# Two token-mixing blocks on one core: which lower parts stand ahead of a handover, and who writes the upper part of a turned input

## The chip, the cores and the metric

The kernel runs on one core of a Trainium2 chip. The metric is the device time of one execution in microseconds (us). The engines are TensorE (PE; PEld is its weight load), VectorE (DVE), ScalarE (ACT), GpSimd (POOL) and SyncE (SP), which issues nearly all loads.

## The reference, cut to what matters

A sequence of 256 tokens of width 1024 goes through two blocks. The first: a gated feed-forward, a token mixing (retention and a neighbourhood attention) and a second gated feed-forward, each with an RMS norm ahead and behind. The second: two layers, each an attention and a feed-forward with a layer norm behind.

```
x = x + 0.5 * rms_norm(swiglu(rms_norm(x)))          # first block: ffn1, mixing, ffn2
...
for i in range(2):                                    # second block
    h = x * (1.0 + scale1) + shift1
    y = moba_attention(h) if i == 0 else diff_attention(h)
    x = layer_norm(ALPHA * x + (1.0 + gate1) * y)
    h = x * (1.0 + scale2) + shift2
    x = layer_norm(ALPHA * x + (1.0 + gate2) * sq_relu_mlp(h))
```

`scale`, `shift` and `gate` are six rows per layer, a product of `silu(c)` with the matrix `ada_w`, which is read along the way. All weights are read once, in float32.

## The kernel before, in words

**Upper and lower parts.** Every float32 operand of a matrix product is split in two: an upper part (a copy rounded to the matmul's format) and a lower part (the operand less the upper part). A product takes three matmuls: upper with upper, the weight's lower with the input's upper, and the weight's upper with the input's lower. For weights these are `wh` and `wl`, for the turned (transposed) input of a stage the two halves of `XX`.

**The weight stream** (class `Stream`). Weights come in slots of two halves of 128 x 1024. A half is loaded into one of 6 `raw` buffers; ScalarE writes `wh` (L115), VectorE `wl` (L93), each into a ring of 8 buffers. `piece` issues one `wh` and appends the half to the list `late`; `flush(n)` issues the open lower parts until `n` are left. A `raw` buffer is free for its next load once its lower part is done; loads are issued by SP in the order of the slots. `use(n)` is called by a stage ahead of its matmuls on slot `n`: it makes the pieces that are missing and then flushes the whole of `late`. `tick`, called after each half that TensorE has used up, makes up to two pieces and flushes.

**Handovers.** Each stage ends in `down_tail`: the last products are done bank by bank (two token halves t, two column halves f; a bank is 128 x 512), so that the norm of token half 0 can run while TensorE does half 1. After each bank, `post.bank` evacuates it. After the last one, `ahead(3)` makes three pieces without any lower part, and `flush(post.low)` issues lower parts until `low` are left: 2 behind an RMS norm (`PostRms`), 1 behind a layer norm (`PostLn`). The next stage begins with `projT`: `use` of its two slots, then for each token half `turn(t)`, which transposes the normed input on TensorE and writes both parts of `XX`, and 24 matmuls of 512 columns. `turn(0)` is already done in the tail (`mid`); `turn(1)` stands right behind it.

`turn_of` has two forms. Without a shift (`c is None`) ScalarE writes the upper part and VectorE the lower one, 128 columns at a time (L597, L598). With a shift ScalarE writes `hf` (L606, eight times); then, for groups of 2, 2 and 4 blocks of 128 columns, the upper part follows, by ScalarE for token half 0 (L612) and by VectorE for half 1 (L610), and the lower part by VectorE (L613).

There are six handovers with a `projT` behind them, numbered here as in the rest of the text: place 1, ffn1 to mixing; place 2, mixing to ffn2; place 3, ffn2 to the first attention; place 4, that attention to its feed-forward; place 5, feed-forward to the second attention; place 6, that attention to its feed-forward. Places 1 to 3 have an RMS norm ahead, 4 to 6 a layer norm; the turns of places 3 to 6 have a shift. Behind `projT`, an attention evacuates `q` by VectorE (L1230 and the lines behind it), a feed-forward of the second block evacuates `u` as `q` by ScalarE and VectorE (L765, L766) and transposes that on TensorE (L771).

Each engine runs its instructions in the order in which the program issues them (manual schedule), so a lower part that is issued early stands ahead of all later work of VectorE.

Of the kernel before, what the change touches and what calls it, by code (L numbers as in the profile page):

```python
# [12 lines left out]
AF = mybir.ActivationFunctionType  # L13
# [35 lines left out]
class Stream:  # L49
# [39 lines left out]

    def flush(self, n=0):  # L90
        while len(self.late) > n:
            wl, raw, wh = self.late.popleft()
            self.nc.vector.tensor_tensor(wl, raw, wh.bitcast(F32), OP.subtract)  # L93

    def next_pos(self):
# [7 lines left out]
    def piece(self, lag=1):  # L103
        nc, i, h = self.nc, self.si, self.half
        raw = self.raw.pop((i, h))
        self.half += 1
        if self.half == 2:
            self.half, self.si = 0, i + 1
        if self.seq[i][0] == "w":
            n = self.wpos[i]  # L110
            assert 2 * n + h < self.done + RING, (n, h, self.done)
            wh = self.pool.tile([128, 1024], F32R, name="wh", bufs=RING)
            wl = self.pool.tile([128, 1024], F32R, name="wl", bufs=RING)
            self.parts[n, h] = (wh, wl)
            nc.scalar.activation(wh, raw, AF.Copy)  # L115
            self.late.append((wl, raw, wh))
            if lag is not None:
                self.flush(lag)
            self.load_to()
        else:  # L120
            self.flush()
            self.ada(self.seq[i][3], h, raw)
            self.load_to()
# [32 lines left out]
    def use(self, n, b):  # L156

        while self.next_pos() <= n + 0.5:
            self.piece()
        self.flush()  # L160
        return [[t.rearrange("p (k f) -> p k f", f=b) for t in self.parts[n, h]] for h in range(2)]

    def release(self, n, h):
# [8 lines left out]
def block_kernel(ctx, tc, A, out):  # L172
    nc = tc.nc
    V, SC, PE, GP = nc.vector, nc.scalar, nc.tensor, nc.gpsimd
# [14 lines left out]
    def w2(name, bufs=None):  # L189
        return work.tile([128, 512], F32, name=name, tag="w2", bufs=4)  # L190
# [395 lines left out]
    def turn_of(src, a, c, alloc=gu):  # L586

        def turn(t):
            ps = [alloc("xt"), alloc("xt")]
            for k in range(8):  # L590
                PE.transpose(ps[k // 4][:, k % 4 * 128:k % 4 * 128 + 128], src[:, t, k * 128:(k + 1) * 128], ident)
            if c is None:
                for i in range(4):
                    for b in range(2):
                        k = 4 * b + i
                        x, h, l = ps[b][:, i * 128:(i + 1) * 128], XX[:, k, 0, TS[t]], XX[:, k, 1, TS[t]]
                        SC.activation(h, x, AF.Copy, scale=a[:, k:k + 1])  # L597
                        V.scalar_tensor_tensor(l, x, a[:, k:k + 1], h.bitcast(F32), op0=OP.mult, op1=OP.subtract)  # L598
                return
            for k0, n in ((0, 2), (2, 2), (4, 4)):  # L600
                if k0 != 2:
                    w = w2("hf").rearrange("p (k s) -> p k s", k=4)
                f = w[:, k0 % 4:k0 % 4 + n]
                for i in range(n):
                    k = k0 + i
                    SC.activation(f[:, i], ps[k // 4][:, k % 4 * 128:k % 4 * 128 + 128], AF.Identity,  # L606
                                  scale=a[:, k:k + 1], bias=c[:, k:k + 1])
                h, l = (XX[:, k0:k0 + n, i, TS[t]] for i in range(2))
                if t:
                    V.tensor_copy(h, f)  # L610
                else:
                    SC.activation(h, f, AF.Copy)  # L612
                V.tensor_tensor(l, f, h.bitcast(F32), OP.subtract)  # L613
        return turn

    class PostRms:

        low = 2
# [19 lines left out]

    class PostLn:

        low = 1

        def __init__(self, accs, gate):
            self.accs, self.gate = accs, gate
# [846 lines left out]
```

## Time and profile before

| | us |
|---|---|
| median of 3 runs | 1288.45 (1286.58 to 1289.17) |
| profiled execution, own time | 1282.29 |
| its span | 1280.3 |
| TensorE busy | 1234.5 (96%) |
| VectorE busy | 932.7 (73%) |
| ScalarE busy | 642.5 (50%) |
| of these, lower parts L93 on VectorE, 392 of them | 467.0 |
| of these, upper parts L115 on ScalarE, 392 of them | 400.2 |

The median is of whole executions, the rows are of one profiled execution. In the chain of work that ended last TensorE has 83%, VectorE 8% (half of it the lower parts, 4%) and ScalarE 3%. A row of a timeline gives the start, the time from the first start to the last end of the merged instructions, engine, line and operation, output and inputs, the count, and in brackets the idle time ahead of it with what ended it.

### The profile page before, as it was taken

Reading aid. Unit: us, or ns where it says so; the run is one execution under the profiler, and the core shown is the slowest. Engines: PE = TensorE matmul, PEld = TensorE weight load, DVE = VectorE, ACT = ScalarE, POOL = GpSimd, SP = SyncE. Lnnn points to the kernel's source line nnn. Section 1 sums busy time; section 2 is a strip of 40 time slices with the busy share of each in tenths; the row PEclk is TensorE's granted clock in tenths of the full one; section 3 lists DMA queues with packets and bytes.
Section 4 is the critical chain, followed back from the end, with each engine's and each line's share of the span. In section 5 each row is a group of like instructions: output and inputs, shape, how many; then the busy total and the mean of one; then the engine's idle time right before and its main releaser. Section 6 shows DMA issues by size and latency. Waiting matters only on the chain.

```text
span 1280.3 us, 18974 instructions
## 1 busy us (share of the span) xinstructions
PE 1234.5 (96%) x7222; PEld 1066.3 (83%) x7222; DVE 932.7 (73%) x1295; ACT 642.5 (50%) x1038; POOL 37.8 (3%) x45
## 2 busy tenths in 40 slices
PE   9999989999999999999999998999998999899997
PEld 7888767888888878887889987999977887899995
DVE  5687866888667678768478668777868977775655
ACT  6553565546455455454456545444644555544440
POOL 0000000320000000000000000000000001000000
PEclk9999999999999999999999999999999999899999
DMA  9788778866566477888454346788765434576650
GB/s 314 259 274 281 236 269 184 251 214 185 196 226 214 148 249 265 287 281 283 147 173 130 126 132 197 254 289 286 263 207 168 129 116 148 179 243 220 230 198 34
DMA packets 167884, 271.68 MB, mean 212 GB/s; under 512 B 15888, under 2 KB 119664, under 8 KB 167792
## 3 DMA queue, kind: packets, MB, share of 16 engines
q1 hardware_dynamic: 161328, 268.36, 64.0%
q10 hardware_dynamic: 6464, 2.10, 1.0%
q8 instruction: 57, 0.93, 0.3%
q14 instruction: 35, 0.29, 0.1%
HBM read 269.37 MB, written 1.05 MB: 211 GB/s over the span
## 4 chain that ended last, share of the span: by engine, by line
PE 83%; DVE 8%; ACT 3%; issue 2%; DMA 2%; POOL 1%; SPq 0%; DVEq 0%; ACTq 0%; POOLq 0%
PE acc L201 22%; PE g L201 20%; PE u L201 14%; DVE wl L93 4%; PE q L201 3%; PE oacc L201 3%; PE k L201 3%; PE v L201 3%; PE yr L201 2%; PE as L201 2%; PE ao L201 1%; ACT hf L606 1%; PE nq L201 1%; PE nk L201 1%; PE rk L201 1%
## 5 line engine op out<-in xcount | busy, mean ns | idle before, releaser
L93 DVE TENSOR_TENSOR wl<-raw,wh 128x1024 fp32r<-128x1024 f32 x392 | 467.0, 1219 | 36.4 <-ACT wh L115 35.5
L115 ACT ACTIVATE wh<-raw 128x1024 fp32r<-128x1024 f32 x392 | 400.2, 1055 | 167.4 <-issue 27.7
L201 PE MATMUL acc<-wh,H 128*128 128x512 f32 x864 | 282.4, 395 | 3.0 <-ACT wh L115 3.0
L201 PE MATMUL g<-wh,XX 128*128 128x512 f32 x832 | 264.2, 392 | 1.6 <-DVE XX L598 1.5
L201 PEld LDWEIGHTS acc<-wh,H 128*128 128x128 f32 x864 | 163.1, 189 | 37.2 <-ACT wh L115 3.9
L201 PEld LDWEIGHTS g<-wh,XX 128*128 128x128 f32 x832 | 156.3, 188 | 35.4 <-DVE XX L598 2.0
L201 PE MATMUL acc<-wl,H 128*128 128x512 f32 x432 | 169.6, 393 | 1.7 <-DVE wl L93 1.7
L201 PE MATMUL g<-wl,XX 128*128 128x512 f32 x416 | 162.1, 390 | 0.8 <-DVE wl L93 0.8
L201 PE MATMUL u<-XX,wh 128*128 128x256 f32 x896 | 162.4, 283 | 0.0
L201 PEld LDWEIGHTS u<-XX,wh 128*128 128x128 f32 x896 | 141.4, 192 | 2.0
L201 PE MATMUL u<-XX,wl 128*128 128x256 f32 x448 | 126.8, 283 | 0.0
L339 DVE SCALAR_TENSOR_TENSOR adacc<-raw,csil,adacc 128x1024 f32<-128x1024 f32 x84 | 108.1, 1287 | 0.8
L201 PEld LDWEIGHTS acc<-wl,H 128*128 128x128 f32 x432 | 81.6, 189 | 18.4 <-DVE wl L93 3.1
L201 PEld LDWEIGHTS g<-wl,XX 128*128 128x128 f32 x416 | 78.2, 188 | 16.9 <-DVE wl L93 1.2
L201 PEld LDWEIGHTS u<-XX,wl 128*128 128x128 f32 x448 | 85.9, 192 | 0.0
L779 ACT ACTIVATE q<-u 128x512 f32<-128x512 f32 x28 | 16.7, 598 | 125.0 <-PE u L201 125.0
L780 DVE TENSOR_TENSOR q<-q,u 128x512 f32<-128x512 f32 x28 | 19.2, 687 | 74.0 <-ACT q L779 74.0
L716 ACT ACTIVATE a<-g,r 128x256 f32<-128x256 f32 x44 | 20.5, 473 | 93.9 <-PE g L201 93.9
L718 DVE SCALAR_TENSOR_TENSOR b<-g,r,a 128x256 f32<-128x256 f32 x44 | 20.9, 483 | 60.5 <-ACT a L716 60.5
L201 PE MATMUL v<-wh,XX 128*128 128x256 f32 (+1 forms) x192 | 48.4, 337 | 6.6 <-DVE XX L610 6.6
L201 PE MATMUL k<-XX,wh 128*128 128x256 f32 x256 | 47.3, 286 | 0.0
L201 PE MATMUL q<-XX,wh 128*128 128x256 f32 x256 | 47.2, 285 | 0.0
(288 smaller groups left out, 1761.6 us busy)
## 6 DMA issues: line engine op xcount, KB each, us to landing
raw<-in_ada_w_dram SPq DMA_DIRECT2D x96, 512.0 KB, 5.0
raw<-in_ffn_w_in_dram SPq DMA_DIRECT2D x176, 256.0 KB, 5.0
raw<-in_mlp_w_up_dram SPq DMA_DIRECT2D x64, 512.0 KB, 4.6
raw<-in_mlp_w_down_dram SPq DMA_DIRECT2D x64, 512.0 KB, 4.9
raw<-in_w_mix_in_dram SPq DMA_DIRECT2D x52, 512.0 KB, 4.9
raw<-in_ffn_w_out_dram SPq DMA_DIRECT2D x44, 512.0 KB, 5.6
raw<-in_moba_w_in_dram SPq DMA_DIRECT2D x24, 512.0 KB, 4.4
raw<-in_diff_w_in_dram SPq DMA_DIRECT2D x24, 512.0 KB, 4.6
```

Source lines behind the costliest of these rows:

```text
L93: self.nc.vector.tensor_tensor(wl, raw, wh.bitcast(F32), OP.subtract)
L115: nc.scalar.activation(wh, raw, AF.Copy)
L201: PE.matmul(o, l, r, start=start, stop=stop, skip_group_check=True)
L339: V.scalar_tensor_tensor(t, w, csil[:, kb:kb + 1], t, op0=OP.mult, op1=OP.add)
L606: SC.activation(f[:, i], ps[k // 4][:, k % 4 * 128:k % 4 * 128 + 128], AF.Identity, scale=a[:, k:k + 1], bias=c[:, k:k + 1])
L716: SC.activation(two(a)[:, t], ps[t][:, 0:256], AF.Silu, scale=r[0][:, t:t + 1])
L718: V.scalar_tensor_tensor(two(b)[:, t], ps[t][:, 256:512], r[0][:, t:t + 1], two(a)[:, t], op0=OP.mult, op1=OP.mult)
L779: SC.activation(q, p, AF.Relu)
L780: V.tensor_tensor(q, q, p, OP.mult)
```

## The change

`late` now remembers the slot of each half, and `use(n)` flushes only the lower parts of slots up to `n`. In the turn with a shift the upper part is written by ScalarE for both token halves. `PostLn.low` is 2.

```diff
     def flush(self, n=0):
         while len(self.late) > n:
-            wl, raw, wh = self.late.popleft()
+            wl, raw, wh, _ = self.late.popleft()
             self.nc.vector.tensor_tensor(wl, raw, wh.bitcast(F32), OP.subtract)
...
             nc.scalar.activation(wh, raw, AF.Copy)
-            self.late.append((wl, raw, wh))
+            self.late.append((wl, raw, wh, n))
...
         while self.next_pos() <= n + 0.5:
             self.piece()
-        self.flush()
+        while self.late and self.late[0][3] <= n:
+            self.flush(len(self.late) - 1)
...
                 h, l = (XX[:, k0:k0 + n, i, TS[t]] for i in range(2))
-                if t:
-                    V.tensor_copy(h, f)
-                else:
-                    SC.activation(h, f, AF.Copy)
+                SC.activation(h, f, AF.Copy)
                 V.tensor_tensor(l, f, h.bitcast(F32), OP.subtract)
...
     class PostLn:
 
-        low = 1
+        low = 2
```

TensorE's, SP's and GpSimd's instructions stand in the same order before and after. On VectorE the order differs in twelve pieces, two at each handover, and on ScalarE in four, at the turns of places 3 to 6. The line numbers of the changed kernel are 1 higher from L161 on and 2 lower behind L612.

VectorE at place 4, from the last work on the normed rows (`v`) to the evacuation of `u` as `q`. Before:

```order
L664 TENSOR_SCALAR v<-v,mv,r 128x512 x2
L93 TENSOR_TENSOR wl<-raw,wh 128x1024 x3
L610 CAST XX<-hf 128x2x128
L613 TENSOR_TENSOR XX<-hf,XX 128x2x128
L610 CAST XX<-hf 128x2x128
L613 TENSOR_TENSOR XX<-hf,XX 128x2x128
L610 CAST XX<-hf 128x4x128
L613 TENSOR_TENSOR XX<-hf,XX 128x4x128
L93 TENSOR_TENSOR wl<-raw,wh 128x1024 x3
L766 TENSOR_TENSOR q<-q,u 128x512 x2
```

After:

```order
L662 TENSOR_SCALAR v<-v,mv,r 128x512 x2
L93 TENSOR_TENSOR wl<-raw,wh 128x1024
L611 TENSOR_TENSOR XX<-hf,XX 128x2x128 x2
L611 TENSOR_TENSOR XX<-hf,XX 128x4x128
L93 TENSOR_TENSOR wl<-raw,wh 128x1024 x5
L764 TENSOR_TENSOR q<-q,u 128x512 x2
```

Two of the three lower parts moved from ahead of the input's parts to behind them, and the three upper parts (CAST) left VectorE.

VectorE at place 2, from the last work on the residual rows (`X`) to the first evacuation of ffn2 (`b`); the row behind the eight lower parts of `XX` is the statistics of the RMS norm. Before:

```order
L637 SCALAR_TENSOR_TENSOR X<-m,r,X 128x512 x2
L93 TENSOR_TENSOR wl<-raw,wh 128x1024 x3
L598 SCALAR_TENSOR_TENSOR XX<-xt,sm,XX 128x128 x8
L699 SCALAR_TENSOR_TENSOR s_4220<-s_1922 128x2
L93 TENSOR_TENSOR wl<-raw,wh 128x1024 x4
L718 SCALAR_TENSOR_TENSOR b<-g,r,a 128x256 x2
```

After:

```order
L635 SCALAR_TENSOR_TENSOR X<-m,r,X 128x512 x2
L93 TENSOR_TENSOR wl<-raw,wh 128x1024
L599 SCALAR_TENSOR_TENSOR XX<-xt,sm,XX 128x128 x8
L697 SCALAR_TENSOR_TENSOR s_4218<-s_1922 128x2
L93 TENSOR_TENSOR wl<-raw,wh 128x1024 x6
L716 SCALAR_TENSOR_TENSOR b<-g,r,a 128x256 x2
```

Here the two lower parts moved past the lower parts of `XX` and past the statistics.

VectorE in the tail ahead of place 4, the first two banks of the layer norm. Before:

```order
L93 TENSOR_TENSOR wl<-raw,wh 128x1024 x3
L652 TENSOR_TENSOR v<-oacc,grow 128x512
L653 SCALAR_TENSOR_TENSOR v<-X,v 128x512
L654 BN_STATS bs<-v 128x6
L652 TENSOR_TENSOR v<-oacc,grow 128x512
```

After:

```order
L93 TENSOR_TENSOR wl<-raw,wh 128x1024 x2
L650 TENSOR_TENSOR v<-oacc,grow 128x512
L651 SCALAR_TENSOR_TENSOR v<-X,v 128x512
L652 BN_STATS bs<-v 128x6
L93 TENSOR_TENSOR wl<-raw,wh 128x1024
L650 TENSOR_TENSOR v<-oacc,grow 128x512
```

One lower part moved from ahead of the first bank to between the first and the second; in the tails ahead of places 1 to 3 it moved behind the first bank's one instruction (L629) in the same way.

## Rows read from the trace of the kernel before

**Rows 1.** The chain that ended last, whole run: start us, us, what.

```profile
645.19 3.40 DVE wl L93 x3
648.85 5.72 PE v L201 x24
...
774.36 10.00 PE u L201 x48
...
793.87 5.47 PE acc L201 x24
799.33 5.75 PE u L201 x48
...
965.61 7.08 PE v L201 x24
...
1092.78 11.18 PE u L201 x48
```

**Rows 2.** Waits of the whole run: total us, times, longest us.

```profile
ACT wh L115 <- PE v L201: 11.4, 7, 4.3
...
PE v L201 <- DVE XX L610: 6.6, 2, 3.6
...
PE u L201 <- DVE XX L610: 5.8, 2, 2.9
```

**Rows 3.** Timeline, place 3: token half 0's turn, then half 1's `hf`.

```profile
637.22 0.81 ACT L606 ACTIVATE hf<-xt,mod,sc 128x128 f32<-128x128 f32 x2 [1.05 <-PE xt L591]
...
638.05 0.42 ACT L612 ACTIVATE XX<-hf 128x256 fp32r<-128x256 f32 x1
...
641.04 0.63 ACT L612 ACTIVATE XX<-hf 128x512 fp32r<-128x512 f32 x1
...
641.71 0.69 DVE L613 TENSOR_TENSOR XX<-hf,XX 128x512 fp32r<-128x512 f32 x1 [1.63 <-ACT XX L612]
...
645.52 2.90 ACT L606 ACTIVATE hf<-xt,mod,sc 128x128 f32<-128x128 f32 x8 [0.43 <-PE xt L591]
```

**Rows 4.** Timeline, places 4, 5, 6: half 1's `hf`; `q` of place 4.

```profile
771.05 2.90 ACT L606 ACTIVATE hf<-xt,m00c,m00a 128x128 f32<-128x128 f32 x8 [2.44 <-PE xt L591]
...
781.74 1.29 DVE L766 TENSOR_TENSOR q<-q,u 128x512 f32<-128x512 f32 x2 [0.61 <-ACT q L765]
...
961.56 2.90 ACT L606 ACTIVATE hf<-xt,m01c,m01a 128x128 f32<-128x128 f32 x8 [2.42 <-PE xt L591]
...
1089.48 2.90 ACT L606 ACTIVATE hf<-xt,m10c,m10a 128x128 f32<-128x128 f32 x8 [2.40 <-PE xt L591]
```

**Rows 5.** Timeline, VectorE in the tail ahead of place 4: second bank.

```profile
756.65 0.69 DVE L652 TENSOR_TENSOR v<-oacc,grow 128x512 f32<-128x512 f32 x1 [0.57 <-PE oacc L201]
```

**Rows 6.** Windows of places 3 and 6: busy us by engine, PEclk, DMA share, GB/s.

```profile
646.00:648.00 2.00, 0.00 (x0) 0.00 (x0) 2.00 (x3) 2.00 (x7) 0.00 (x0) 1.00 0.28 36
...
1093.00:1095.00 2.00, 2.00 (x5) 1.62 (x6) 1.93 (x6) 0.32 (x1) 0.00 (x0) 0.50 1.10 341
```

**Rows 7.** Timeline, place 2: loads of SP, TensorE's wait, ScalarE's upper parts.

```profile
447.99 2.02 SPq L79 DMA_DIRECT2D raw<-in_ffn_w_in_dram  x4
...
450.55 0.90 PE L201 MATMUL g<-wh,XX 128*128 128x512 f32 x2 [1.54 <-DVE XX L598]
...
455.51 4.84 ACT L115 ACTIVATE wh<-raw 128x1024 fp32r<-128x1024 f32 x5
```

**Rows 8.** DMA issues of 445 to 465, then 208 to 232: KB, us to landing.

```profile
raw<-in_ffn_w_in_dram SPq DMA_DIRECT2D x8, 256.0 KB, 4.7
...
prow<-in_smalls_dram SPq DMA_DIRECT2D x1, 512.0 KB, 3.5
...
raw<-in_w_mix_in_dram SPq DMA_DIRECT2D x7, 512.0 KB, 7.3
```

**Rows 9.** Timeline, place 1: half 1's first upper and lower parts.

```profile
212.48 0.62 ACT L597 ACTIVATE XX<-xt,sm 128x128 fp32r<-128x128 f32 x2 [1.83 <-PE xt L591]
...
214.04 0.60 DVE L598 SCALAR_TENSOR_TENSOR XX<-xt,sm,XX 128x128 fp32r<-128x128 f32 x2
```

## The prediction

> **What bounds the kernel now.** I read three views. The busy shares come first: TensorE is busy for 96% of the span, so only its few idle stretches can be won. The chain of work that ended last comes second: it runs over TensorE almost everywhere, but at six places it leaves it for a run of lower parts on VectorE. These are the handovers between stages, numbered 1 to 6 in the section on the kernel. Third is the view of waits: at places 3 to 6 TensorE's first matmul on the second token half waits for `XX` from VectorE (L610), four times, 12.4 us in all [rows 2]. In the chain of place 3 [rows 1] the reader sees three lower parts (3.40 us, so 1.13 each) from 645.19, and only behind them the `XX` for the matmuls that start at 648.85. ScalarE has had the turned input since 645.52 [rows 3]. So the wait is one for place in VectorE's queue, not for data.
>
> **The change part by part.** (a) `use` no longer finishes lower parts of later slots. The order shows two consequences at all six handovers: two of the three lower parts move behind the lower parts of `XX`, and in the tail ahead one moves behind the first bank's first work. (b) The upper part of the turned input at places 3 to 6 goes from VectorE to ScalarE. (c) `low = 2` behind the layer norms (places 4 to 6) leaves two lower parts open instead of one; without it (a) would free only one there.
>
> *The new rhythm of places 3 to 6.* The first token half already runs it, upper parts by ScalarE [rows 3]: counted from the first `hf` at 637.22, the first upper part is done after 1.25 us, the third after 4.45 (641.67), and the third lower part after 5.18 (642.40). TensorE does 24 matmuls of 512 columns in 5.47 at its high clock [rows 1], 0.228 each. It could run the first twelve from 1.25 on; the thirteenth needs the third upper part (4.45), the fifteenth its lower part (5.18). From there ten are left: 2.28, and about 0.16 until the last one's end as the chain counts it. So the half ends 7.6 us after the first `hf`.
>
> Place 3: `hf` starts at 645.52, so the half ends at 653.1 instead of 648.85 + 5.72 = 654.6 [rows 1, 3]: **1.4 us** won.
>
> At places 4 to 6 a layer norm stands ahead, and the lower part moved into its tail has no room: between two banks VectorE idles 0.57 us there [rows 5], a lower part takes 1.13. Everything up to the second half's `hf` comes about 0.5 us later. In the RMS tails (places 1 to 3) the banks lie as far apart and VectorE does one instruction on each, so the cover holds and I cost it at nothing; without it each place would pay the same 0.5.
>
> Place 5: `hf` at 961.56 + 0.5, the half ends at 969.7 instead of 965.61 + 7.08 = 972.7 [rows 1, 4]: **3.0**. Nearly half of that is the clock: 7.08 here against 5.72 at place 3 for the same 24 matmuls.
>
> Place 4: the third lower part of `XX` ends at 771.05 + 0.5 + 5.2 = 776.7. Behind it VectorE now has five lower parts (before: three) ahead of `q` (L766): 5.7, then 1.3 for `q` itself, 783.7. TensorE's transposes of `q` began where the 48 matmuls of the chain end, about 784.2 [rows 1, 4]. TensorE is done earlier and waits; the gain is **0.5**. Here the stall comes back, and what is late next is `q`.
>
> Place 6: the same sum, with four lower parts: 1089.48 + 0.5 + 5.2 + 4.5 + 1.3 = 1101.0, against 1092.78 + 11.18 = 1104.0 less 0.2, so 1103.8: **2.8**. It is more than at place 4, since one lower part fewer stands ahead of `q` and more of the old time was low clock: 11.18 against 10.00 for the same 48 matmuls.
>
> *The clock.* Place 3 idled 2.9 us in one piece [rows 2] and the granted clock stayed at 1.00 (2.4 GHz); at place 6 it was 0.50 (1.2 GHz) after two idle pieces around the transposes [rows 6]. The new schedule leaves about 2.4 us in two pieces at places 4 and 5, and less at 6. I take the high level; if the low level stays, place 5 gives 2.2 and place 6 gives 1.8. The Trainium skill (TensorE: Matmul & The Clock Gate, "What you observe" and "What's actually happening") says that the moment of the change varies from run to run, since it depends on where in a free-running window the work falls. By that rule the two clock terms could go either way in each execution, and the sum would lie between 6 and 8 us; no row here shows two executions.
>
> *ScalarE's share.* Eight `hf` took 2.90, with the upper parts between them 4.45: the `wh` queued behind come 1.55 later. Cover: those `wh` already wait for TensorE to release the ring (11.4 us behind `v` alone [rows 2]). Without that cover it is 1.5 at each of four places, inside the ends below.
>
> *Place 2.* A lower part also frees its `raw` buffer. The load into the second buffer was issued with the group at 447.99 [rows 7]; now it stands behind the statistics of the RMS norm, whose squares ScalarE does directly ahead of the five `wh` at 455.51. TensorE's wait of 1.54 [rows 7] goes, so these squares end at about 453.9 and the second lower part at 455.0. Two transfers of this kind, issued half a microsecond apart, take 4.7 to land, the fastest in that stretch 3.5 [rows 8]: 459.0 to 460.2. The fifth `wh` used to start at 455.51 + 4 x 0.97 = 459.4, and the first activation of the feed-forward stands behind it. So the gain of 1.5 is taken back by one late load: +0.4 to -0.8, I take **-0.2**. The Trainium skill (DMA: Bandwidth & Descriptors, "Anatomy of one DMA") gives about 2.0 us fixed plus bytes by 436 GB/s for transfers that GpSimd issues; an estimate from that is 3.2 us for this load, and by it the place would gain 0.5 and the sum be 0.7 higher. The rows here are slower.
>
> *Place 1.* The alternating L597 and L598 could start at about 212.9 instead of 214.04 [rows 9]: 1.1 won. Here the late load meets the transfer of `bias` and takes 7.3 [rows 8], and the work behind it on ScalarE belongs to a chain in which VectorE is nearly full. Between -0.6 and +1.1, I take **+0.3**.
>
> Sum: 0.3 - 0.2 + 1.4 + 0.5 + 3.0 + 2.8 = 7.8 us. Against the profiled execution's own time that is 1282.29 - 7.8 = 1274.5. The median of the runs shown is 1288.45, 6 us above the profiled one, so the forecast for a median is 1288.45 - 7.8 = **1280.7**. The low ends add up to -0.6 - 0.8 + 1.2 + 0 + 2.2 + 1.8 = 3.8, the high ones to 1.1 + 1.5 + 1.4 + 1.0 + 3.5 + 3.3 = 11.8: 1276.7 to 1284.7.
>
> **The rivals.** *The stall returns at every place as at place 4.* The lower parts are only deferred; if their pile-up behind `XX` holds the next evacuation everywhere, places 3 to 6 give 0.5 each: 1288.45 - 2.0 = 1286.4. For it: VectorE's queue is the reason of the present stall. Against it: at place 3 the order has seven lower parts (7.9 us) between the last one of `XX` (650.7) and the next evacuation (`q`, L1230). They end at 658.6, and the 48 matmuls that fill `q`'s bank (5.75 [rows 1]) end at 653.1 + 5.75 = 658.9: just in time.
>
> *Slower: the late loads win.* Two `raw` buffers come free later at each of six places: at place 3 the second at 650.7 + 1.1 = 651.8 instead of 645.19 + 2.27 = 647.5. If loads then land in 7.3 us as at place 1 [rows 8], place 2's comes at 455.5 + 7.3 = 462.8, 3.4 after ScalarE wanted it; place 1 the same, and places 3 to 6 lose 1.3 each (half of 7.3 - 4.7, the rest hidden): 12.0 lost, 7.7 won at places 3 to 6, 1292.7. It decides from the point where a load takes over 5 us to land and TensorE needs what ScalarE has queued behind its `wh`. For it: place 2 stands near that point. Against it: only place 1 has the transfer that made it 7.3.
>
> *More than forecast.* If the load at place 2 lands in time, the tails of the layer norms cost nothing and the clock never falls, the high ends hold: 1288.45 - 11.8 = 1276.7.
>
> That the change does not do what it says is excluded by the order.
>
> **How the numbers follow.** Forecast 0.66, stall returns 0.17, slower 0.07, more 0.10. A measurement of this kernel can tell about 0.2%, 2.6 us. Faster by more: 0.66 + 0.10 and a third of the second case, 0.81; within: 0.12; slower: 0.07. The range takes the forecast's bounds, the case above and most of the stall returning, and 1.5 us for the spread of medians: 1275.2 to 1287.4.
>
> **What would show it.** In the profile after: one lower part instead of three ahead of `XX` at each handover; TensorE's waits on L610 gone and its first matmul of places 3 to 6 about 2 us earlier relative to `hf`; the granted clock at 1.00 there; a new wait of TensorE for `q` at place 4; at place 2 a wait of `wh` for a load of `ffn_w_in`. I am wrong if the clock still falls at places 5 and 6, if ScalarE's `wh` wait for loads at places 3 to 6, or if TensorE's waits move to the next evacuation instead of going.

## The result and the profile after

The changed kernel takes 1278.22 us in the median of six runs (1275.71 to 1280.31), the kernel before beside it 1286.07 (1281.79 to 1289.17): ratio 0.9937, 95% interval 0.9923 to 0.995, so 7.9 us less where 7.8 were forecast. For the median itself 1280.7 was forecast, from a kernel before at 1288.45 in its first three runs. The profiled execution after takes 1277.45, its span is 1275.7. The forecast sum is right; several of its terms are not, as the places show.

The page after, busy time and share of the span for each engine, then the chain of work that ended last by line:

```profile
PE 1235.5 (97%) x7216; PEld 1064.2 (83%) x7222; DVE 929.5 (73%) x1283; ACT 648.1 (51%) x1050; POOL 39.7 (3%) x45
...
PE acc L202 23%; PE g L202 20%; PE u L202 12%; PE q L202 3%; PE k L202 3%; PE v L202 3%; DVE wl L93 3%; PE oacc L202 2%; PE yr L202 2%; PE as L202 2%; ACT hf L607 1%; PE ao L202 1%; DMA raw<-in_ffn_w_in_dram 1%; PE nq L202 1%; PE nk L202 1%
```

TensorE's waits after (total us, times, longest us):

```profile
PE g L722 <- DVE b L716: 3.6, 1, 3.6
...
PE u L202 <- ACT XX L610: 2.1, 4, 0.9
...
PE u L769 <- DVE q L764: 1.3, 3, 0.8
...
PE v L202 <- DVE grow L393: 1.2, 1, 1.2
...
PE v L202 <- ACT XX L610: 0.9, 1, 0.9
```

The 12.4 us of waits for the upper part on VectorE [rows 2] are gone; ScalarE's upper part is waited for instead, 0.9 at the longest; at place 5 the wait of 1.2 is put down to `grow`, which VectorE writes directly ahead of the lower parts of `XX`. Larger than before are the waits for `q` (L764), as forecast, for `b` (L716) at place 2, and those for `v` at the heads of places 4 to 6 (2.9 before, 4.1 after), which come from the tails.

**By place.** Since TensorE's instructions stand in the same order in both kernels, the same matmul can be looked up in two traces, and the difference of its starts shows what was won or lost up to there. Each entry of the table is the change of this difference across a place, against the profiled execution before (negative is won). What differs ahead of place 1 is left out, up to 3.9 us in kernels that are alike there. In the kernel after it is 3.9: 1.5 where the clock is low at 133 us, and most of the rest in the first 11 us, where the same matmul takes 0.78 instead of 0.48; its first loads are within 0.3 us of those of the kernel before. So the spans of the two profiled executions, 1280.3 and 1275.7, lie only 4.6 apart, though the places give 8.4. Two stretches that no edit touches stand apart: "605" holds one TensorE wait for `ada` in ffn2, "att" the attention around 1047 us of the second layer.

| kernel | 1 | 2 | 605 | 3 | 4 | 5 | att | 6 | tails 4, 5, 6 |
|---|---|---|---|---|---|---|---|---|---|
| after | -1.44 | +2.27 | +0.04 | -1.26 | -1.08 | -3.32 | -1.51 | -3.38 | 0.48, 0.30, 0.46 |
| after, second execution | -1.46 | +2.97 | -1.59 | -1.25 | -1.07 | -2.23 | -0.02 | -3.39 | 0.47, 0.31, 0.44 |
| (b)+(c), no (a) | -0.19 | -0.02 | +0.05 | -0.30 | -0.24 | -0.31 | -0.03 | -2.88 | 0, 0.28, 0 |
| (a)+(c), no (b) | -0.80 | +2.75 | -1.56 | -2.15 | -2.02 | -3.63 | -0.01 | -4.49 | 0.47, 0.82, 0.40 |
| (a)+(b), no (c) | -1.47 | +2.74 | -1.57 | -1.28 | -2.22 | -2.88 | +1.35 | -3.79 | 0.47, 0.31, 0.38 |
| (a) alone | -1.03 | +2.96 | -1.60 | -2.11 | -2.51 | -0.89 | -1.51 | -3.67 | 0.48, 0.33, 0.46 |

The stretch at 133 us, in the kernel before and in the kernel after (columns as below):

```profile
133.00:136.00 3.00, 3.00 (x17) 2.50 (x16) 3.00 (x4) 2.21 (x4) 0.00 (x0) 1.00 0.98 356
```

```profile
133.00:136.00 3.00, 2.72 (x6) 2.15 (x7) 2.52 (x4) 2.75 (x3) 0.00 (x0) 0.50 0.47 138
```

Windows of the kernel before: 439 to 497 is place 2, then 605, 4, 5, att and 6. Columns: length, busy us of PE, PEld, DVE, ACT, POOL, then the granted clock as a share of full speed, DMA share, GB/s.

```profile
439.52:497.12 57.60, 54.94 (x252) 44.29 (x250) 41.82 (x57) 32.21 (x55) 1.25 (x2) 1.00 0.68 227
600.00:623.85 23.85, 22.55 (x116) 18.48 (x115) 13.46 (x16) 10.05 (x12) 0.00 (x0) 0.93 0.58 195
...
760.64:804.92 44.28, 40.08 (x247) 35.24 (x247) 36.19 (x50) 23.26 (x39) 0.54 (x1) 0.96 0.55 174
951.18:984.04 32.86, 28.13 (x169) 24.53 (x170) 23.70 (x37) 19.32 (x32) 0.54 (x1) 0.95 0.40 122
1037.38:1066.27 28.89, 26.92 (x179) 23.37 (x178) 20.47 (x55) 16.53 (x50) 4.41 (x4) 0.94 0.40 120
1081.41:1135.74 54.33, 49.95 (x305) 44.51 (x304) 40.75 (x55) 28.80 (x43) 0.55 (x1) 0.94 0.66 209
```

The same work in the kernel after:

```profile
441.94:501.81 59.87, 56.17 (x251) 45.42 (x250) 42.18 (x57) 32.60 (x55) 2.17 (x2) 0.97 0.66 219
604.70:628.59 23.89, 22.59 (x117) 18.48 (x116) 13.45 (x16) 10.06 (x12) 0.00 (x0) 0.93 0.58 183
...
764.59:807.79 43.20, 39.72 (x247) 34.00 (x248) 35.16 (x47) 24.51 (x42) 0.54 (x1) 1.00 0.58 190
954.35:983.89 29.54, 27.24 (x168) 23.36 (x170) 22.59 (x34) 20.70 (x35) 0.54 (x1) 1.00 0.47 148
1037.14:1064.52 27.38, 25.40 (x179) 21.85 (x178) 20.46 (x55) 16.55 (x50) 4.42 (x4) 1.00 0.40 125
1080.11:1131.06 50.95, 48.19 (x306) 42.36 (x304) 39.64 (x52) 30.18 (x46) 0.56 (x1) 1.00 0.69 224
```

The granted clock has two levels, 1.00 and 0.50; a share between them is the mean of a window. Where it falls, TensorE does the same matmuls slower: at place 6 TensorE idled 4.38 of 54.33 us before and 2.76 of 50.95 after, so 1.6 of the 3.4 won is idle time and 1.8 is busy time, 49.95 against 48.19. A clock of 0.94 over 28.89 us means that up to 28.89 x 0.06 = 1.7 us were lost; the entries of "605" and "att" differ from each other in steps of 1.4 to 1.6 and in nothing else.

### The profile page after: what moved, and what is told of

Its sections match the earlier page's. It is cut to its first block, busy times and chain, and to the rows that moved or that the text cites. A ratio compares the mean times of both kernels' runs of the same rounds, so it can differ in the third digit from the quotient of the medians.

```text
span 1275.7 us, 18960 instructions
## 1 busy us (share of the span) xinstructions
PE 1235.5 (97%) x7216; PEld 1064.2 (83%) x7222; DVE 929.5 (73%) x1283; ACT 648.1 (51%) x1050; POOL 39.7 (3%) x45
## 4 chain that ended last, share of the span: by engine, by line
PE 81%; DVE 8%; ACT 4%; issue 3%; DMA 2%; POOL 1%; SPq 0%; DVEq 0%; ACTq 0%; POOLq 0%
PE acc L202 23%; PE g L202 20%; PE u L202 12%; PE q L202 3%; PE k L202 3%; PE v L202 3%; DVE wl L93 3%; PE oacc L202 2%; PE yr L202 2%; PE as L202 2%; ACT hf L607 1%; PE ao L202 1%; DMA raw<-in_ffn_w_in_dram 1%; PE nq L202 1%; PE nk L202 1%
## 5 line engine op out<-in xcount | busy, mean ns | idle before, releaser
L202 PE MATMUL g<-wh,XX 128*128 128x512 f32 x832 | 266.9, 396 | 0.0
L716 DVE SCALAR_TENSOR_TENSOR b<-g,r,a 128x256 f32<-128x256 f32 x44 | 20.9, 482 | 64.9 <-ACT a L714 64.9
```

The source lines that it names most:

```text
L202: PE.matmul(o, l, r, start=start, stop=stop, skip_group_check=True)
L716: V.scalar_tensor_tensor(two(b)[:, t], ps[t][:, 256:512], r[0][:, t:t + 1], two(a)[:, t], op0=OP.mult, op1=OP.mult)
```

## The experiments

The theory at the start: lower parts ahead of `XX` in VectorE's queue cause the stall, so (a) carries the gain; (b) costs a little, (c) costs in the tails. The rivals: (b) carries it, or (c) is needed. Medians stand beside the kernel before run with them.

**(a) undone.**

```diff
-        while self.late and self.late[0][3] <= n:
-            self.flush(len(self.late) - 1)
+        self.flush()
```

> Part (a) undone: a call of use finishes every open lower part again; parts (b) and (c) stay. Theory 1 (the time went because lower parts of later slots stood in VectorE's queue ahead of the lower parts of XX, so (a) carries the gain): the three lower parts (1.13 each) are back ahead of XX at places 3 to 6, and of the 7.85 us only a little is left. With the upper parts on ScalarE the upper part of XX no longer queues behind the lower ones, so some 0.35 a place, 1.4 in all, and up to 1.5 more if the clock falls less often: 3 us at most below the kernel before, about 1283 to 1286. Place 2 must be back at its old time: the fifth wh doesn't wait for a load, and TensorE's wait of 3.62 is not there. Rival (the gain is that the upper part left VectorE, part (b)): within 2 us of the kernel after, about 1278 to 1280.

1279.75 (ratio 0.9953, interval 0.9937 to 0.9968): 6 us less than before, where at most 3 were expected; by the median alone the rival (1278 to 1280) would have it. By the trace (a) carries places 1 and 3 to 5: without it they give 0.2 to 0.3 each. Place 6 is where the theory fell: -2.88 with the three lower parts still in the way, since the clock, low there in the one trace of the kernel before, is high in this one. TensorE's idle time went from 4.38 to 51.45 - 47.67 = 3.78 and its clock stayed at 1.00:

```profile
1081.71:1133.16 51.45, 47.67 (x306) 42.51 (x304) 39.84 (x52) 30.05 (x46) 0.55 (x1) 1.00 0.69 223
```

What (b) does to the stall shows at place 3 of the same kernel: one wait of 2.9 [rows 2] becomes two.

```profile
647.79 0.50 PE L201 MATMUL v<-wh,XX 128*128 128x512 f32 x1 [0.89 <-ACT XX L609]
648.13 0.40 PE L201 MATMUL v<-wl,XX 128*128 128x512 f32 x1
649.98 0.74 PE L201 MATMUL v<-wh,XX 128*128 128x512 f32 x2 [1.46 <-DVE XX L610]
```

The trace accounts for 3.6 us of the 6; the rest has no place in it. The kernel before shows a mean clock of 0.987 over all its runs beside these experiments, 0.990 in its profiled execution and 0.992 in this kernel's runs, so its typical execution loses more to the clock than the one that was traced; where, no row shows. The same bears on the change as a whole. At a mean clock of 0.990 six runs of the kernel before took 1282.1 to 1286.2 us and two of the kernel after 1277.4 and 1280.3. An estimate from these few is that some 4 us of the gain are left at an equal clock, and that the rest comes with the clock, 0.987 before and 0.992 after.

**(b) undone.**

```diff
-                SC.activation(h, f, AF.Copy)
+                if t:
+                    V.tensor_copy(h, f)
+                else:
+                    SC.activation(h, f, AF.Copy)
```

> Part (b) undone: the upper part of the second half's turned input goes to VectorE again, (a) and (c) stay. Theory 1: (b) is worth nothing by itself and even costs. With ScalarE doing three upper parts between the hf, the last lower part of XX ends 5.2 us behind the first hf (0.97 an hf, and 0.3 to 0.5 for each upper part between them); with the upper parts on VectorE directly ahead of their lower parts the last one ends some 4 behind it. So each of places 3 to 6 ends about 0.6 to 1.2 earlier than in the kernel after, and the five wh behind come 1.5 earlier: 2 to 4 us below the kernel after, about 1274 to 1276. Rival (b carries the gain): the sum gives back 3 us or more, 1281 or above, and TensorE waits again for XX at places 3 to 6 by about 3 us each.

1273.94 (0.9903, 0.9886 to 0.992): some 4 us below the kernel after, as the theory has it. Places 3, 4 and 6 win 0.89, 0.94 and 1.11 more; place 5 wins 0.31 more, and its tail gives 0.52 back, since `grow` landed later in that execution. VectorE at place 3:

```profile
646.54 0.29 DVE L611 CAST XX<-hf 128x256 fp32r<-128x256 f32 x1
646.87 0.42 DVE L614 TENSOR_TENSOR XX<-hf,XX 128x256 fp32r<-128x256 f32 x1
647.24 0.29 DVE L611 CAST XX<-hf 128x256 fp32r<-128x256 f32 x1
647.57 0.43 DVE L614 TENSOR_TENSOR XX<-hf,XX 128x256 fp32r<-128x256 f32 x1
648.64 0.43 DVE L611 CAST XX<-hf 128x512 fp32r<-128x512 f32 x1 [0.64 <-ACT hf L607]
649.10 0.69 DVE L614 TENSOR_TENSOR XX<-hf,XX 128x512 fp32r<-128x512 f32 x1
```

A cast costs VectorE 0.29 to 0.43; on ScalarE the same cost 0.42 to 0.63 and delayed the next `hf` (an `hf` takes 0.36 here, eight in 2.90 [rows 3]; the 0.97 of the expectation is what a `wh` takes). From the first `hf` (645.70) to the first `q` matmul (652.47) this kernel needs 6.77, the kernel after 7.64. With (a) done, (b) is a loss.

**(c) undone**, and **(a) alone** ((b) and (c) undone).

```diff
     class PostLn:
...
-        low = 2
+        low = 1
```

> Part (c) undone: one lower part instead of two left open behind a layer norm; (a) and (b) stay. Theory 1 (the lower part that moved into the layer norm's tail costs about 0.4 there three times, and stands again ahead of q at place 4, and in the kernel after the input's second half waits for ScalarE and not for VectorE): one more lower part goes to its old place ahead of the turned input, where VectorE waits for ScalarE anyway. Places 4 to 6 keep their gain and the tails give 0.47 + 0.3 + 0.46 back: about 1.2 us below the kernel after, 1277. Rival ((c) is needed, as without it (a) frees one lower part only): XX stands behind one lower part more at places 4 to 6, 1.1 each: 3.4 less 1.2 above the kernel after, 1280.5.

> Part (a) alone on the kernel before: use finishes only what its slots need; upper parts of the second half by VectorE, one lower part open behind a layer norm. Theory: (a) carries the gain and needs neither (b) nor (c): places 3 to 6 gain 2.0, 2.5, 3.0 and 4 us, the tails cost 1.2, place 1 gains 1.0 and place 2 loses 2.3: 9.0 below the kernel before, 1277 or less. Rival ((c) is needed, since with one lower part open behind a layer norm (a) frees one alone, and two stand ahead of XX at places 4 to 6): 1.1 less at each of the three, about 1281.

Without (c): 1277.38 (0.993, 0.9915 to 0.9945), 1 us below the kernel after, within what the runs can tell. Place 4 wins 1.1 more (one lower part fewer ahead of `q`), place 6 0.4, place 5 0.4 less; the tails did not come back, against the expectation, so it is (a) that moved the lower part into them. With (a) alone: 1278.11 (0.994, 0.9922 to 0.9958), nearer to the theory (1277) than to the rival (1281), but place 5 wins 0.89 instead of 3.63: one lower part stands ahead of `XX`, TensorE idles 3.66 there instead of 2.52, and the clock falls. So (c) pays where VectorE does the upper part, at places 5 and 6 (2.7 with the clock, and 0.8); place 4 shows 0.5 less with it, in a trace in which the clock fell there. Where ScalarE does the upper part, `XX` waits for ScalarE anyway.

**Place 2: the lower parts ahead of the statistics.** In the kernel after with one line more at places 1 and 2:

```diff
                     turn(1)
+                    st.flush()
                     rms.token(0)
```

> The kernel after, and at places 1 and 2 the remaining lower parts are finished right behind the two turned halves, ahead of the statistics of the RMS norm instead of behind them. Theory 1 (at place 2 the change lost 2.3 us, since the second raw buffer came free 2 to 3 us later, its load landed after the fifth wh wanted it, which waited 2.29, TensorE idled 3.62 in one piece, and its clock fell: about 0.7 of late load and 1.6 of clock): the load is issued some 2 us earlier, the wait of 2.29 goes, and 1.5 to 2.5 us come back: about 1276 in the median. Rival 1 (the clock fell there by chance and not by the idle piece): only 0.7 comes back, 1277.5. Rival 2 (the statistics themselves are late then, and with them the normed tiles): no gain, 1278 or above.

1273.4 (0.99, 0.9884 to 0.9917), less than the 1276 expected: place 2 went from +2.27 to -1.74. The chain of the kernel after at place 2 (start, us, what) shows the loss, the lower part, then the load, then the fifth `wh`:

```profile
456.42 1.24 DVE wl L93
...
458.13 4.16 DMA raw<-in_ffn_w_in_dram
...
462.39 1.06 ACT wh L115
...
463.46 0.57 ACT L714
...
466.20 0.55 PE g L722 x3
```

With the line, ScalarE runs the five `wh` in one piece and the activation of ffn2 begins 2 us earlier:

```profile
456.61 4.84 ACT L115 ACTIVATE wh<-raw 128x1024 fp32r<-128x1024 f32 x5
461.47 1.28 ACT L714 ACT_TABLE_LOAD   x1
```

The swing of 4.0 is more than what had been lost: TensorE's 1.54 at the head of the place [rows 7] is now won and kept, and the clock stays high. Place 1 gives 1.11.

**Place 2: the clock.** In the kernel after, TensorE idles 3.62 us ahead of the transposes of `b`, and right behind it the clock is low:

```profile
467.00:470.60 3.60, 3.60 (x10) 2.79 (x10) 3.60 (x5) 0.98 (x2) 0.00 (x0) 0.54 0.94 297
```

To tell the idle piece from the late load, the gap was filled with 12, then 20 matmuls whose result nobody reads:

```diff
+            if j == 0 and gain == G_F2POST:
+                w = acc("fill")
+                for i in range(12):
+                    mm(w, XX[:, i % 8, 0, 0:128], XX[:, 0:2, 0, :], True, True)
             p = ps[0]
```

> The kernel after, with 12 matmuls of 128x512 more at place 2, into a bank that nobody reads (work that adds nothing to the result). TensorE takes them between the last matmul of the projection and the transposes of b, where it idles 3.62 to 4.4 in every kernel with the late load; they take about 12 x 0.228 = 2.7 us and leave about 1 us idle. Theory (of the 2.3 us that place 2 lost, 1.6 to 1.8 are the clock that falls behind the idle piece): the load and the fifth wh are as late as before, the transposes start at the same place, and the clock at the matmuls behind them stays at the high level: the place is 1.6 to 1.8 shorter, about 1276.5 in the median. Rival (the clock falls by chance or with the late load itself, not by the idle piece): it falls all the same, and the place keeps its 2.3 to 3.0.

> The kernel after with 20 instead of 12 matmuls in the gap of place 2 (they add nothing to the result). With 12 the gap ran to 4.4 us and 1.59 of it stayed idle; the clock fell right behind it all the same, as it did behind the pure idle pieces of 3.62 to 4.4. 20 of them take 20 x 0.24 = 4.8 us and close the gap, and may hold the transposes of b up by some 0.4. Theory (it is the idle piece ahead of the transposes; one of 1.3 to 1.6 can bring the fall too, as the one of 1.30 at 605 us does in some executions and not in others): with no idle piece the clock stays at 1.00 behind the gap, and place 2 is 1.2 to 1.8 us shorter than in the kernel with 12, about 1276. Rival (the fall is bound to the late load or to what the engines do there, not to TensorE's idling): it falls again, and the place loses 2.9 as with 12, or 3.4.

With 12, 1.59 us stayed idle and the clock fell all the same (place 2: +2.98), so this run alone spoke for the rival:

```profile
459.94 2.88 PE L202 MATMUL fill<-XX 128*128 128x512 f32 x12
464.42 1.02 PE L726 MATMUL g<-cst,b 128*128 128x128 f32 x4 [1.59 <-DVE b L716]
...
465.00:468.00 3.00, 3.00 (x10) 2.42 (x10) 3.00 (x4) 1.58 (x3) 0.00 (x0) 0.52 0.85 292
```

With 20 nothing idles and the clock stays:

```profile
461.92 4.70 PE L202 MATMUL fill<-XX 128*128 128x512 f32 x20
466.46 0.60 PE L726 MATMUL g<-cst,b 128*128 128x128 f32 x4
...
465.00:468.00 3.00, 3.00 (x17) 2.49 (x16) 3.00 (x4) 2.70 (x4) 0.00 (x0) 1.00 0.98 363
```

Place 2 loses 1.10 instead of 2.98 with the load just as late: up to the transposes both runs have lost 1.4. Behind them the run with 12 loses another 1.6, and so do both executions of the kernel after: this is the clock, and the idling of TensorE brings it about. The remaining 0.3 between the two runs is not the clock's: the four transposes take 0.60 right behind the 20 matmuls and 0.94 behind an idle piece at the high clock in the kernel before. The medians (1276.94 and 1278.87) don't tell the two apart; the traces do, in one execution each.

**The tails.** On the kernel after:

```diff
         w = [st.use(n, D) for n in ns]
+        st.flush()
```

> The kernel after, and a call in down_tail finishes every open lower part right behind its use, as before the change. Theory: the lower part that moved behind the tail's first bank costs 0.47, 0.30 and 0.46 in the three layer norm tails of the trace after; ahead of the tail VectorE has room for it. So 1.2 us below the kernel after, about 1277. Rival: ahead of the tail it holds up the bank's first work by the same amount, and the time stays at that of the kernel after, 1278.2. The two lie within what the medians can tell; the profile decides, by how far the xt matmuls of places 4 to 6 stand from the last stage's.

1274.91 (0.9926, 0.9907 to 0.9946). Tails 4 and 6 lose nothing now (0.03 and -0.01). Tail 5 still loses 0.48, and loses 0.28 with (a) undone: there VectorE waits for `grow` from the load of `ada_b`, 4.4 to 4.9 us in these executions, and not for a lower part.

**`q` ahead of three lower parts** (up to four may stay open in the feed-forwards of places 4 and 6), on the kernel after. The call, cut from the edit; `projT` hands the number on to the pieces that are made in it:

```diff
-        projT(ps, turn, lambda: start_now(hidden01(ps)))
+        projT(ps, turn, lambda: start_now(hidden01(ps)), 4)
```

> The kernel after, and in the feed-forwards behind a layer norm (places 4 and 6) up to four lower parts stay open while the turned input is used, so that the first evacuation q goes ahead of three of them on VectorE. Theory: at place 4 the change won 1.1 of the trace and stopped there since q stands behind five lower parts; with three fewer ahead of it the place gains 1 to 2 more and place 6 some 0.5: 1.5 to 2.5 us below the kernel after, about 1276. Rival (the lower parts left for later hold up the next u, as four of them are needed by the third and fourth weight tiles): the gain is given back one piece later, and the time is that of the kernel after.

1275.55 (0.9913, 0.9896 to 0.9929). Place 4 wins 2.60 instead of 1.08, place 6 3.76 instead of 3.38; nothing is given back behind. VectorE at place 4, in the kernel after:

```profile
780.11 5.76 DVE L93 TENSOR_TENSOR wl<-raw,wh 128x1024 fp32r<-128x1024 f32 x5
785.78 1.28 DVE L764 TENSOR_TENSOR q<-q,u 128x512 f32<-128x512 f32 x2
```

and with the edit, where `q` waits for ScalarE alone:

```profile
775.30 2.35 DVE L93 TENSOR_TENSOR wl<-raw,wh 128x1024 fp32r<-128x1024 f32 x2
778.97 1.29 DVE L769 TENSOR_TENSOR q<-q,u 128x512 f32<-128x512 f32 x2 [1.31 <-ACT q L768]
780.17 5.76 DVE L93 TENSOR_TENSOR wl<-raw,wh 128x1024 fp32r<-128x1024 f32 x5
```

**All of it together** ((b) undone and the three additions), and the same with the line at place 2 alone.

> Four edits on the kernel after: the upper part of the second half by VectorE again, open lower parts finished ahead of the RMS statistics (places 1 and 2) and ahead of the tails, and four lower parts open at places 4 and 6. Singly the first two gave about 4.5 and 4.9 us by their medians against the kernel after, in part by the clock; the tails are thought to be worth 1.2 and the last edit 2. If they add: 4.5 + 4.9 + 1.2 + 1 (the last edit and the first work on the same wait, so half of it) = 11.6 below the kernel after, about 1267. Rival: the first two gained by the same thing (fewer stretches at the low clock) and don't add: about 1271.

> The combination once more, with the lower parts ahead of the RMS statistics at place 2 alone and not at place 1. In the trace of the combination place 1 won 0.16 and in the kernel after 1.44: finishing the lower parts early there takes back what the change gives. Theory: 0.8 to 1.3 us below the combination (1269.19), about 1268. Rival (place 1 with the upper part on VectorE wins less anyway, 0.80 and 1.03 in the two kernels that have it): 0.6 less, 1268.6; the medians cannot tell these two apart, the offsets in the trace can.

1269.19 (0.9864, 0.9844 to 0.9885) and 1268.48 (0.9866, 0.9843 to 0.989): 16 to 18 us below the kernel before, 9 below the kernel after, between theory and rival of the first. The second cannot be told from it. What was supposed of place 1 is not borne out: both win 1.3 at its head and give 0.7 to 1.1 back 30 us later, most of it in a wait of TensorE for `dec` (1.10 and 0.66), with the line at place 1 and without it. In the second the trace shows why: the fifth `wh` waits for its load, ScalarE writes `R` behind it, VectorE waits for `R`, and `dec` stands behind that on VectorE.

```profile
226.27 1.06 ACT L118 ACTIVATE wh<-raw 128x1024 fp32r<-128x1024 f32 x1 [3.61 <-DMA raw<-in_w_mix_in_dram]
...
227.63 0.54 DVE L1094 TENSOR_TENSOR cosr<-cst,R 128x256 f32<-128x256 f32 x1 [2.84 <-ACT R L1093]
```

The kernel after has the same wait, shorter, and there nobody is held up by it:

```profile
228.69 1.06 ACT L115 ACTIVATE wh<-raw 128x1024 fp32r<-128x1024 f32 x1 [1.66 <-DMA raw<-in_w_mix_in_dram]
```

Eight of the executions profiled here, two of them of the kernel after, are of kernels that are alike up to the end of place 1. In five of these the load is waited for by 1.6 to 1.8 us and the place gives 1.3 to 1.5; in the other three by 3.1 to 3.4, and it gives 0.8 to 1.0. In the first of the two combinations the load is waited for by 2.06 only, and what holds `dec` up further stays open.

**The kernel after once more.**

> The kernel after once more, unchanged, for a second profiled execution of it. Theory (what the change gives at a place repeats, and the clock beside the idle pieces does not): places 1, 3, 5 and 6 and the tails show the same offsets as in the first to within 0.1 us (wins of 1.44, 1.26, 3.32 and 3.38, losses of 0.47, 0.30 and 0.46), and differences come only in steps of about 1.6 at the stretches where the clock can fall: behind the idle 1.30 at 605, in the attention around 1047, at places 4 and 5. Place 2 loses 2.3 to 3.0 again with its clock falling again. Rival (the place sums are chance too): they differ by half a microsecond or more without a change of clock. The median should be 1278 within 2.

1276.68 (0.993, 0.991 to 0.9949), by this ratio 9 us below the kernel before, so that 7.9 against 7.8 is closer than two measurements of the same change are. Its entries of the table repeat to within 0.03 at places 1, 3, 4, 6 and the tails. Place 5 differs by 1.09, and there the clock fell this time:

```profile
950.86:981.49 30.63, 28.33 (x169) 24.66 (x171) 22.61 (x34) 20.57 (x35) 0.54 (x1) 0.94 0.46 144
```

Place 2 differs by 0.70 (idle piece 4.35 instead of 3.62, the clock low in both), 605 and att by one step each. So the sums of places 3, 4 and 6 are the change's, and the clock behind the idle pieces is the execution's. How late a load lands is the execution's, too: it moves place 2 here, and place 1 in the kernels that are alike there.

## Why the prediction was right, and where it was not

- **Place 3, 1.4 forecast, 1.26 measured.** The rhythm was read correctly: the first `q` matmul stands 7.64 behind the first `hf`, and the half was forecast to end 7.6 behind it. That the same rhythm makes (b) a cost was not worked out; the undone (b) shows it.
- **Place 4, 0.5 net; 1.08 - 0.48 = 0.6.** The stall comes back on `q` behind five lower parts as forecast, and three fewer of them ahead of it free 1.5 more.
- **Place 5, 3.0 net; 3.32 - 0.30 = 3.0, and 1.9 in the second execution.** The sum took the high clock and named 2.2 for the low one. Of the seven profiled executions with all three parts at this place, the clock was high in three and low in four: the first agreed by luck. That the clock still falls at place 5 is one of the prediction's own signs of being wrong.
- **Place 6, 2.8 net; 3.38 - 0.46 = 2.9, and 2.95 again.** Idle and clock as forecast, the clock high in every kernel that has (a) or (b). But (b) and (c) alone bring 2.88, of which 2.3 is busy time at the higher clock (49.95 against 47.67), and that the clock is low there before is known from one execution.
- **Tails, 0.5 each.** Right for tails 4 and 6. In tail 5 the moved lower part costs 0.3 in both executions, though `grow` comes 0.16 later than before in the one and 0.27 earlier in the other; where that lower part is not in the way ((a) undone, the tails mended), `grow` comes 0.28 and 0.47 later and the tail loses the same.
- **Place 2, -0.2 forecast, -2.3 and -3.0 measured: the step that failed.** The load was sized well: it took 4.16 to land, forecast up to 4.7, and the transposes of `b` come 0.7 later than before in the first execution, inside the forecast's -0.8, and 1.4 later in the second. The estimate from the Trainium skill (DMA: Bandwidth & Descriptors, "Anatomy of one DMA", for transfers that GpSimd issues) was 3.2 for this load, which SyncE issues; the row is slower. What was not in the sum is that the two idle pieces of before, 1.54 and 1.03, would become one of 3.62, and that the clock falls behind it: 1.6 us in each execution, and none with the gap filled. The clock was weighed at places 4 to 6 alone and put at nothing here.
- **Place 1, 0.3 forecast, 1.4 measured.** The term was mis-sized. The head of the place won 1.25, 1.1 forecast; the 0.8 charged for the late load with `bias` in its way did not come due in either execution of the kernel after. The mechanism is there all the same: in three other executions of kernels that are alike up to here that load came later still, and a wait for `dec` left 0.8 to 1.0.
- **The sum** came out since place 1 (+1.1) stood against place 2 (-2.1 or -2.8), and chance steps of the clock (att -1.51, 605 -1.59) lie in each pair of traces; the two traces of the kernel after give -8.4 and -6.8 by places, -4.6 and -5.6 by spans, beside the medians' -7.9. That the sum met the median to a tenth is luck.

That the clock could go either way in each execution holds at place 5 and not at place 6, where it was high in all 13 executions after a change. Behind the same idle 1.30 at 605 it fell in 5 of 14. The prediction took this from the rule of the Trainium skill (TensorE: Matmul & The Clock Gate, "What's actually happening") that the moment of the change depends on where in a free-running window the work falls; the runs agree that it varies. Of the rivals, the return of the stall came true at place 4 alone. The late loads cost at place 2, and at place 1 in some executions.

## What to carry to other kernels

Before an operation is moved past a lower-priority one, ask what the moved instruction frees: here a lower part freed a load buffer, and the place that lost is the one where the next load was needed soonest. Give work to another engine only if that engine is not the one waited for next: with the queue cleared, the upper part was better on VectorE. Weigh idle pieces of TensorE by whether they merge, and compare two traces place by place, so that chance steps of the clock don't pass for an edit's effect.

## What the runs showed of the hardware

- A fall of TensorE's clock behind an idle piece cost 1.4 to 1.6 us at place 2, at 605 and in the attention around 1047, and 1.1 at place 5. Behind pieces of 3.62 to 4.38 at place 2 it came in all seven executions that had one; behind 1.59 (with busy work ahead) in the one that had it; behind 1.30 in 5 of 14; at place 2 with pieces up to 1.54 in none of five. The length of the piece does not decide alone: in the kernel before the clock stayed high behind 2.9 at place 3 and was low behind 2.9 at places 4 and 6, where another idle piece (1.31 and 0.54) had ended 4.0 us before it did; this is one execution.
- What a low clock costs can be hidden: with the tails mended, place 4 ran at 0.96 instead of 1.00 and won the same (1.07 and 1.08), since TensorE waited for `q` anyway (idle 2.61 instead of 3.48).
- Between two executions of one program, the entries of places 3, 4 and 6 repeat to within 0.03 us; what differs elsewhere is the clock and when a load lands.
- How late one and the same load lands differs by execution: at place 1 ScalarE waited 1.56 to 3.44 us for it in eight executions of kernels that are alike up to there.
